# The low part of every fourth weight chunk made by an accumulating DMA instead of a VectorE subtraction

## The chip, the cores and the metric

The kernel runs on one core of a Trainium2 chip. The metric is the device time of one execution in microseconds (us). A core has a matrix engine (TensorE, PE in the profile; its weight loads are PEld), three engines for elementwise work (VectorE or DVE, ScalarE or ACT, GpSimd or POOL), and SyncE (SP), which here only issues DMAs. Every engine works through its own instruction stream in order. GpSimd and ScalarE can issue DMAs too. All DMAs of the core run on the same 16 DMA engines. TensorE writes into PSUM; everything else lives in SBUF, a memory of 128 partitions.

## The reference

One decoder layer on 256 rows of width 2048, in float32:

```
h = RMSNorm(x)
[cB|cC|cX|q|k|v|g_conv|g_attn] = h @ w_in                    # 2048 x 19456
A = (cB * causal_dwconv3(cC * cX)) @ w_conv_out              # 2048 x 2048
B = dilated_window_attention(rope(norm(q)), rope(norm(k)), v) @ w_attn_out   # 1024 x 2048
x = x + (sigmoid(g_conv) * A + sigmoid(g_attn) * B) @ w_merge_out            # 2048 x 2048
h = RMSNorm(x)
[g|u] = causal_dwconv3(h @ w_up)                             # 2048 x 11264
x = x + (silu(g) * u) @ w_down                               # 5632 x 2048
```

There are 24 heads of 128 in three groups of different dilation. The weights are 340 MB, all read once.

## The kernel before

**Two parts for each factor.** The products are made from float32r operands. Every weight and every activation is written as the sum of two float32r numbers, hi and lo, and each product takes three of the four combinations: hi by hi, hi by lo, lo by hi. For a weight chunk, hi is ScalarE's rounding of the raw float32 values to float32r (line 109), and lo is VectorE's difference raw minus hi (line 110).

**The weight stream.** All weights are one list of 656 chunks, numbered in the order in which TensorE uses them. A chunk is 512 KB, 4 KB in each partition (the first 16 are half of that). SyncE loads it into a buffer `raw` (line 99); there are 5 raw buffers. The split makes `whi` and `wlo`, with 4 buffers each (`SPLIT_BUFS`). While chunk i is at work, the program issues loads up to chunk i + 7 (`LOAD_AHEAD` of 8 counts the chunk itself) and splits up to chunk i + 2 (`SPLIT_AHEAD` of 3), but an instruction starts only when its buffer is free: hi of chunk i can be written when TensorE has read hi of chunk i - 4, and a raw buffer is loaded again when both split instructions of its chunk have read it.

**The products.** Chunks belong to blocks. A block of kind F has 256 weight columns and 4 chunks, and the weights stand in the array: per 128 rows and 128 columns one matmul with hi against both parts of the activations (line 185, 512 wide) and one with lo against their hi part (line 186, 256 wide). A block of kind T has 512 columns, 2 x 128 rows a chunk, and the weights stream past the activations in three matmuls (lines 189, 190 and 191; 190 uses lo). A block of kind T has 8 or 11 chunks; the attention-output blocks (F) have 2. Each block collects into one of two PSUM buffers and is then evacuated by ScalarE and VectorE (`fsum`, line 296 and 297), scaled, convolved, gated, and split for the next product.

**What sets the order.** The instruction order on each engine is put together by the framework's scheduler from the order in which the program issues work and its estimate of when inputs are ready. Work beside the stream (transposes, attention, convolution) is queued by `after(n, ...)` and issued n chunks later. In the up stage (blocks ug and uv, F) the convolution's two ScalarE instructions (line 311), the SiLU (line 614) and the split of the result (line 303) stand between the stream's instructions on ScalarE.

In the functions below `split_to` is the one that the change touches. `last["act"]` and `last["dve"]` hold the latest split instruction of each engine; `behind` uses them to issue side work after it.

Of the kernel before, what the change touches and what calls it, by code (L numbers as in the profile page):

```python
# [11 lines left out]
F32 = mybir.dt.float32  # L12
F32R = mybir.dt.float32r
I32 = mybir.dt.int32
AF = mybir.ActivationFunctionType
ALU = mybir.AluOpType
# [35 lines left out]
SPLIT_BUFS = 4  # L52
LOAD_AHEAD = 8
SPLIT_AHEAD = 3


def _round_bits(v, bits):
# [5 lines left out]
def hybrid_block(ctx: ExitStack, tc: tile.TileContext, x, positions, mix_norm, w_in, conv_mix_w,  # L63
                 w_conv_out, q_norm, k_norm, w_attn_out, w_merge_out, ffn_norm, w_up, ffn_conv_w,
                 w_down, out):
    nc = tc.nc
# [15 lines left out]
    def bank(name):  # L82
        return ps_one.tile([P, 512], F32, tag="one", name=name)

    # ---- the weight stream: chunks of rows by columns, 4 KiB a partition, loaded and split ahead.
    # A weight is the exact sum of two float32r parts, as the activations are.
    chunks, xt = [], []
    x_before = {min(2 * i, 13) for i in range(8)}
    raws, splits = {}, {}
# [2 lines left out]
    def load_to(n):  # L92
        while issued["load"] < min(n, len(chunks)):
            i = issued["load"]
            if i in x_before:
                xt.append(load_x(k2("x"), len(xt), FW))
            w, r0, kc, c0, cw = chunks[i]
            raws[i] = wpool.tile([P, kc, cw], F32, tag="raw", name="raw", bufs=RAW_BUFS)
            nc.sync.dma_start(raws[i], w[r0:r0 + kc * P, c0:c0 + cw].rearrange("(k p) n -> p k n", p=P))
            issued["load"] += 1  # L100

    def split_to(n):
        while issued["split"] < min(n, len(chunks)):
            i = issued["split"]
            load_to(i + 1)
            raw = raws.pop(i)
            hi = wpool.tile(list(raw.shape), F32R, tag="whi", name="whi", bufs=SPLIT_BUFS)
            lo = wpool.tile(list(raw.shape), F32R, tag="wlo", name="wlo", bufs=SPLIT_BUFS)
            last["act"] = nc.scalar.activation(hi, raw, AF.Copy)  # L109
            last["dve"] = nc.vector.tensor_tensor(lo, raw, hi.bitcast(F32), op=ALU.subtract)  # L110
            splits[i] = (hi, lo)
            issued["split"] += 1

    last = {}
# [28 lines left out]
    blocks, steps = [], []  # L143
# [10 lines left out]
    def interleave(n):  # L154
        half = n // 2
        for seq in (steps, chunks):
            head = seq[:n]
            seq[:n] = [head[i // 2 + (i % 2) * half] for i in range(n)]
            seq[n - 3], seq[n - 2] = seq[n - 2], seq[n - 3]

    def run_blocks():
        for i, (b, k, kc) in enumerate(steps):
# [8 lines left out]
            pump()  # L171
            load_to(i + LOAD_AHEAD)
            split_to(i + SPLIT_AHEAD)
            hi, lo = splits.pop(i)
            end = k + kc >= kts
# [16 lines left out]
            if end:  # L192
                b["evac"](ps)

    # ---- constants
    ident = cpool.tile([P, P], F32, name="ident")
    make_identity(nc, ident)
    ones = cpool.tile([P, P], F32, name="ones")
    nc.vector.memset(ones, 1.0)

    # the clock of TensorE rises while it works: it starts before the first data are there
    warm = ps_sc.tile([P, 4, S], F32, tag="sc", name="warm")
    for i in range(WARM):
        nc.tensor.matmul(warm[:, 0, :P], ones, ones, start=True, stop=True)
# [37 lines left out]
        nc.vector.tensor_copy(fconv.rearrange("p k c -> p (k c)"), tq[:, :264])  # L242
        nc.vector.tensor_copy(cols[:, 16:80], tq[:, 264:328])

    # ---- RMSNorm: rows' squares are summed here, 1/rms goes onto what the products give
    def row_squares(xs, ssq, c):
        junk = k2("junk")
        n = xs.shape[2]
        for t in range(NT):
            nc.scalar.activation(junk[:, :n], xs[:, t, :], AF.Square, accum_out=ssq[:, t, c:c + 1])  # L250
# [73 lines left out]
    X = [None] * 8  # L324
    x_src = src_of(X)

    # ---- branch A: the gated short convolution
    cy, m1 = [None] * 8, [None] * 8
    keep = {}

# [43 lines left out]
            nc.vector.tensor_tensor(m1[nb], m1[nb], gconv[nb], op=ALU.mult)  # L374
        return evac

    # ---- branch B: attention
    rot = {}

    def rope_tables():  # L380
# [190 lines left out]
                    n += 1 + t  # L571
        return evac

    # ---- merge, residual, feed-forward
    mg = [None] * 8

    def ev_attn_out(nb):
# [24 lines left out]
    act = {}  # L602
# [24 lines left out]
                nc.sync.dma_start(out_v[:, t, nb * CW:(nb + 1) * CW], x2[nb][:, t])  # L627
        return evac

    # ---- the order of the products  # L630
    W_in, W_co, W_ao, W_mo, W_up, W_dn = (w[0] for w in (w_in, w_conv_out, w_attn_out, w_merge_out, w_up, w_down))
    for nb in range(8):
        block(W_in, COL_CC + nb * FW, 0, KT, "F", x_src, ev_cc(nb), "cc", 4 if nb else 2)
# [32 lines left out]
        for nb in range(4):  # L666
            block(W_dn, nb * CW, b0 * FW, 2 * (b1 - b0), "T", a_src, ev_down(nb, b1 == NB), "dn")

    # ---- start: x comes in by columns between the weights of the first two blocks, whose steps
    # alternate, so that each piece of x serves both  # L670
    interleave(2 * KT // 2)
    ssq1 = cpool.tile([P, NT, 8], F32, name="ssq1")
    load_to(SPLIT_AHEAD)
    r1 = rb1 = None
# [5 lines left out]
    with tc.issue_after(first_gains().ins):  # L680
        split_to(1)
    h0, l0 = transposed(xt[0], 0, 0, X, "xT")
    with tc.issue_after(h0.ins), tc.issue_after(l0.ins):
        split_to(2)
# [33 lines left out]
```

## Time and profile before

| | |
|---|---|
| time, median of two runs | 1882.42 us (1882.35 to 1882.49) |
| span of the profiled execution, first to last instruction | 1874.8 us |
| mean granted TensorE clock in it | 0.998 |
| TensorE busy | 1864.8 us, 99% |
| TensorE weight loads busy (beside the matmuls) | 1595.4 us, 85% |
| VectorE busy | 1197.5 us, 64% |
| ScalarE busy | 936.8 us, 50% |
| GpSimd busy | 9.0 us |
| DMA: HBM read, share of the weight queue | 344.24 MB, 57.6% of 16 engines' time |

The profiled execution's own time is its span; what lies around the span is not recorded. A row of groups reads: line, engine, operation, output<-inputs, count | busy us, mean ns of one | idle us of the engine just before, and what ended it. A row of the timeline reads: start in us from the span's start, duration in us, engine, line, operation, and in brackets the idle time before it and what ended that. The matmuls are pipelined, so the distance from one start to the next is the better measure of one.

### The profile page before, as it was taken

The page shows a single profiled execution, that of the slowest core. Times are in us where ns is not written, and L with a number is a line of the kernel's source. Part 1 is how long each engine was busy: PE and PEld are TensorE (multiplying, and loading weights), DVE is VectorE, ACT ScalarE, POOL GpSimd, SP SyncE. Part 2 cuts the span into 40 slices and gives each one's busy share as a digit, 9 for nine tenths or more (in the row PEclk, how much of TensorE's full clock was granted, in tenths as well). Part 3 has the DMA queues.
Part 4 walks back from the last instruction along what each step waited for, and adds up shares of the span by engine and source line. Part 5 has one row for each costly group of instructions (what it writes and reads, how often), then busy time and mean ns, then how long its engine had stood idle before and what let it go on. Part 6 is the DMA issues. An engine that isn't in the chain of part 4 may idle for free.

```text
span 1874.8 us, 25347 instructions
## 1 busy us (share of the span) xinstructions
PE 1864.8 (99%) x9807; PEld 1595.4 (85%) x9807; DVE 1197.5 (64%) x1599; ACT 936.8 (50%) x1208; POOL 9.0 (0%) x24
## 2 busy tenths in 40 slices
PE   8999999999999999999999999999999999999998
PEld 7888888888888888888888888888888888888887
DVE  5776666555566575666476756777764467777643
ACT  6444444444555454555465545555553345555432
POOL 1000000000000000000000000000000000000000
PEclk9999999999999999999999999999999999999999
DMA  8555565656555644555545665655655565665563
GB/s 253 181 189 183 189 186 185 190 182 190 186 185 180 192 155 148 189 185 188 180 135 170 212 212 182 191 191 191 191 191 191 192 190 186 185 189 183 191 215 121
DMA packets 279480, 348.00 MB, mean 186 GB/s; under 512 B 10959, under 2 KB 209663, under 8 KB 279360
## 3 DMA queue, kind: packets, MB, share of 16 engines
q1 hardware_dynamic: 279104, 346.07, 57.6%
q8 instruction: 77, 1.26, 0.3%
q0 software_dynamic: 224, 0.30, 0.1%
q14 instruction: 43, 0.35, 0.1%
q10 hardware_dynamic: 32, 0.01, 0.0%
HBM read 344.24 MB, written 2.10 MB: 185 GB/s over the span
## 4 chain that ended last, share of the span: by engine, by line
PE 99%; DMA 0%; ACT 0%; SPq 0%; DVE 0%; DVEq 0%; issue 0%
PE ps_ug L185 9%; PE ps_uv L185 9%; PE ps_ug L186 4%; PE ps_uv L186 4%; PE ps_dn L190 4%; PE ps_dn L191 4%; PE ps_dn L189 4%; PE ps_cx L185 3%; PE ps_cc L185 3%; PE ps_co L185 3%; PE ps_gc L185 3%; PE ps_ga L185 3%; PE ps_cb L185 3%; PE ps_k L189 2%; PE ps_v L189 2%; PE ps_q L189 2%
## 5 line engine op out<-in xcount | busy, mean ns | idle before, releaser
L110 DVE TENSOR_TENSOR wlo<-raw,whi 128x1024 fp32r<-128x1024 f32 (+1 forms) x656 | 794.0, 1211 | 591.4 <-ACT whi L109 588.5
L109 ACT ACTIVATE whi<-raw 128x1024 fp32r<-128x1024 f32 (+1 forms) x656 | 688.0, 1049 | 840.0 <-PE ps_dn L191 134.3
L185 PE MATMUL ps_ug<-h,whi 128*128 128x512 f32 x704 | 247.5, 395 | 0.0
L185 PE MATMUL ps_uv<-h,whi 128*128 128x512 f32 x704 | 247.4, 395 | 0.0
L186 PE MATMUL ps_ug<-h,wlo 128*128 128x256 f32 x704 | 197.7, 281 | 0.0
L186 PE MATMUL ps_uv<-h,wlo 128*128 128x256 f32 x704 | 197.4, 280 | 0.0
L185 PEld LDWEIGHTS ps_uv<-h,whi 128*128 128x128 f32 x704 | 132.0, 187 | 30.9
L185 PEld LDWEIGHTS ps_ug<-h,whi 128*128 128x128 f32 x704 | 132.0, 187 | 30.9
L191 PE MATMUL ps_dn<-whi,act 128*128 128x512 f32 x352 | 137.0, 389 | 0.0
L189 PE MATMUL ps_dn<-whi,act 128*128 128x512 f32 x352 | 137.0, 389 | 0.0
L190 PE MATMUL ps_dn<-wlo,act 128*128 128x512 f32 x352 | 137.0, 389 | 0.0
L186 PEld LDWEIGHTS ps_ug<-h,wlo 128*128 128x128 f32 x704 | 133.0, 189 | 0.1
L186 PEld LDWEIGHTS ps_uv<-h,wlo 128*128 128x128 f32 x704 | 133.0, 189 | 0.0
L185 PE MATMUL ps_cc<-xT,whi 128*128 128x512 f32 x256 | 93.0, 405 | 0.1
L185 PE MATMUL ps_ga<-xT,whi 128*128 128x512 f32 x256 | 92.6, 402 | 0.0
L185 PE MATMUL ps_cx<-xT,whi 128*128 128x512 f32 x256 | 92.4, 403 | 0.2 <-ACT whi L109 0.2
L185 PE MATMUL ps_co<-conv,whi 128*128 128x512 f32 x256 | 90.8, 399 | 0.0
L185 PE MATMUL ps_gc<-xT,whi 128*128 128x512 f32 x256 | 90.8, 399 | 0.0
L185 PE MATMUL ps_cb<-xT,whi 128*128 128x512 f32 x224 | 79.5, 399 | 0.0
L189 PEld LDWEIGHTS ps_dn<-whi,act 128*128 128x128 f32 x352 | 66.1, 188 | 13.9
L190 PEld LDWEIGHTS ps_dn<-wlo,act 128*128 128x128 f32 x352 | 66.1, 188 | 13.7
L191 PEld LDWEIGHTS ps_dn<-whi,act 128*128 128x128 f32 x352 | 66.1, 188 | 13.6
(219 smaller groups left out, 3265.1 us busy)
## 6 DMA issues: line engine op xcount, KB each, us to landing
raw<-in_w_in SPq DMA_DIRECT2D x296, 512.0 KB, 3.5
raw<-in_w_up SPq DMA_DIRECT2D x176, 512.0 KB, 3.6
raw<-in_w_down SPq DMA_DIRECT2D x88, 512.0 KB, 4.0
raw<-in_w_conv_out SPq DMA_DIRECT2D x32, 512.0 KB, 3.5
raw<-in_w_merge_out SPq DMA_DIRECT2D x32, 512.0 KB, 3.5
raw<-in_w_attn_out SPq DMA_DIRECT2D x16, 512.0 KB, 3.5
raw<-in_w_in SPq DMA_DIRECT2D x16, 256.0 KB, 4.1
x<-in_x SPq DMA_DIRECT2D x8, 256.0 KB, 5.6
```

The source lines that it names most:

```text
L109: last["act"] = nc.scalar.activation(hi, raw, AF.Copy)
L110: last["dve"] = nc.vector.tensor_tensor(lo, raw, hi.bitcast(F32), op=ALU.subtract)
L185: nc.tensor.matmul(ps[:, m, :], hi[:, j, w_], xs, start=first, stop=False)
L186: nc.tensor.matmul(ps[:, m, :S], lo[:, j, w_], xs[:, :S], start=False, stop=last)
L189: nc.tensor.matmul(ps[:, m, :], sh, hi[:, j, :], start=first, stop=False)
L190: nc.tensor.matmul(ps[:, m, :], sh, lo[:, j, :], start=False, stop=False)
L191: nc.tensor.matmul(ps[:, m, :], sl, hi[:, j, :], start=False, stop=last)
```

## The change

From chunk 60 on, every chunk whose number is divisible by four gets its lo part in another way. ScalarE writes the negated rounding of raw into `wlo` (a second activation, with scale -1), and GpSimd issues a DMA from `raw` into `wlo` that adds to what is there: raw minus the rounding. VectorE's subtraction is left out for these chunks. Chunks 60, 64, ..., 652 are 149. In a block of kind F with four chunks it is always the first chunk of the block.

```
+DMA_FROM = 60
+DMA_EVERY = 4
...
             last["act"] = nc.scalar.activation(hi, raw, AF.Copy)
-            last["dve"] = nc.vector.tensor_tensor(lo, raw, hi.bitcast(F32), op=ALU.subtract)
+            if i >= DMA_FROM and i % DMA_EVERY == 0:
+                last["act"] = nc.scalar.activation(lo, raw, AF.Copy, scale=-1.0)
+                nc.gpsimd.dma_start(lo, raw, accum_op=ALU.add)
+            else:
+                last["dve"] = nc.vector.tensor_tensor(lo, raw, hi.bitcast(F32), op=ALU.subtract)
```

The rest of the diff takes out comments. The lines of the changed kernel are numbered 2 higher at the loads and the first split instruction (99 is 101, 109 is 111), the negated copy is 113, the DMA 114, the subtraction 116, and lines behind it are 6 higher (185 is 191, 311 is 317).

How the scheduler places the new instructions is shown at three places of the up stage. First ScalarE, from the evacuation of a ug block to that of the next uv block, before:

```order
L296 ACTIVATE upa<-ps_ug 128x512
L109 ACTIVATE whi<-raw 128x1024
L311 ACTIVATE upc<-up,fconv 128x256 x2
L109 ACTIVATE whi<-raw 128x1024
L614 ACTIVATE upc<-upc 128x512
L109 ACTIVATE whi<-raw 128x1024 x2
L296 ACTIVATE upa<-ps_uv 128x512
```

The same stretch of ScalarE in the changed kernel:

```order
L302 ACTIVATE upa<-ps_ug 128x512
L111 ACTIVATE whi<-raw 128x1024
L317 ACTIVATE upc<-up,fconv 128x256 x2
L113 ACTIVATE wlo<-raw 128x1024
L111 ACTIVATE whi<-raw 128x1024
L620 ACTIVATE upc<-upc 128x512
L111 ACTIVATE whi<-raw 128x1024 x2
L302 ACTIVATE upa<-ps_uv 128x512
```

The negated copy of the next block's first chunk does not follow its whi directly: the two convolution instructions stand between. Of the 149 copies 42 stand so, 90 follow their whi directly, and 17 have another instruction between, in ten of them the sigmoid of a gate (line 371).

Second TensorE, from the last matmul of a uv block into the next ug block, with what each instruction waits for (DVE: VectorE, Activation: ScalarE), before:

```order
L186 MATMUL ps_uv<-h_9757,wlo 128x256
L185 MATMUL ps_ug<-h_9228,whi 128x512 [waits DVE_49,Activation_49]
L186 MATMUL ps_ug<-h_9228,wlo 128x256 [waits DVE_49]
L185 MATMUL ps_ug<-h_9228,whi 128x512
L186 MATMUL ps_ug<-h_9228,wlo 128x256
```

And in the changed kernel, where DMASW stands for a DMA that GpSimd issued:

```order
L192 MATMUL ps_uv<-h_9841,wlo 128x256
L191 MATMUL ps_ug<-h_9306,whi 128x512 [waits DVE_49,Activation_49]
L192 MATMUL ps_ug<-h_9306,wlo 128x256 [waits DMASW3_49]
L191 MATMUL ps_ug<-h_9306,whi 128x512
L192 MATMUL ps_ug<-h_9306,wlo 128x256
```

TensorE's own order is the same; the second matmul of the block, the first with wlo, waits for the landing of the accumulation instead of VectorE.

Third SyncE, loads of w_up, before (DMAHW: the load that filled the buffer earlier):

```order
L99 DMA raw<-in_w_up 128x4x256 [waits DMAHW6_49,DVE_49]
L99 DMA raw<-in_w_up 128x4x256 [waits DMAHW7_49,DVE_49]
L99 DMA raw<-in_w_up 128x4x256 [waits DMAHW0_49,DVE_49]
L99 DMA raw<-in_w_up 128x4x256 [waits DMAHW1_49,DVE_49]
L99 DMA raw<-in_w_up 128x4x256 [waits DMAHW2_49,DVE_49]
```

And in the changed kernel:

```order
L101 DMA raw<-in_w_up 128x4x256 [waits DMAHW5_49,DMASW3_49]
L101 DMA raw<-in_w_up 128x4x256 [waits DMAHW7_49,DVE_49]
L101 DMA raw<-in_w_up 128x4x256 [waits DMAHW0_49,DVE_49]
L101 DMA raw<-in_w_up 128x4x256 [waits DMAHW2_49,DVE_49]
L101 DMA raw<-in_w_up 128x4x256 [waits DMAHW1_49,DMASW4_49]
```

Every fourth load now waits until an accumulation has landed, since that reads the raw buffer to its end, and the loads behind it on SyncE wait with it.

## The prediction

> **What bounds the kernel now.** First the page of the profile: busy time by engine, and the chain that ended last.
>
> ```profile
> span 1874.8 us, 25347 instructions
> PE 1864.8 (99%) x9807; PEld 1595.4 (85%) x9807; DVE 1197.5 (64%) x1599; ACT 936.8 (50%) x1208; POOL 9.0 (0%) x24
> PE 99%; DMA 0%; ACT 0%; SPq 0%; DVE 0%; DVEq 0%; issue 0%
> ```
>
> TensorE is busy for all but 10.0 us of the span and the chain is TensorE alone. Next, where those 10.0 us lie: stretches of the span, PE busy in the second column, DMA share next to last.
>
> ```profile
> 0.00:60.00 60.00, 54.80 (x299) 47.00 (x300) 38.85 (x65) 39.26 (x84) 6.29 (x19) 0.94 0.76 234
> 1116.00:1360.00 244.00, 244.00 (x1382) 213.91 (x1381) 177.78 (x234) 135.34 (x181) 0.00 (x0) 1.00 0.60 190
> 1730.00:1874.80 144.80, 139.98 (x643) 116.31 (x642) 74.58 (x78) 55.98 (x59) 0.00 (x0) 1.00 0.53 175
> ```
>
> 5.2 us stand at the start and 4.8 us at the end, so the stretch that the change touches has nothing to give back. VectorE and ScalarE are not the limit. The groups say how they stand idle:
>
> ```profile
> L110 DVE TENSOR_TENSOR wlo<-raw,whi 128x1024 fp32r<-128x1024 f32 (+1 forms) x656 | 794.0, 1211 | 591.4 <-ACT whi L109 588.5
> L109 ACT ACTIVATE whi<-raw 128x1024 fp32r<-128x1024 f32 (+1 forms) x656 | 688.0, 1049 | 840.0 <-PE ps_dn L191 134.3 <-PE ps_ug L185 94.0 <-PE ps_uv L185 86.1
> ```
>
> VectorE waits for ScalarE's whi; ScalarE waits for TensorE to finish with an older weight buffer. So the split runs a fixed distance ahead of TensorE. The timeline of an up block shows that distance.
>
> ```profile
> 1303.97 0.39 PE L185 MATMUL ps_uv<-h,whi 128*128 128x512 f32 x1
> ...
> 1306.83 1.06 ACT L109 ACTIVATE whi<-raw 128x1024 fp32r<-128x1024 f32 x1 [1.23 <-PE ps_uv L185]
> ...
> 1307.79 0.90 ACT L311 ACTIVATE upc<-up,fconv 128x256 f32<-128x256 f32 x2
> 1307.92 1.23 DVE L110 TENSOR_TENSOR wlo<-raw,whi 128x1024 fp32r<-128x1024 f32 x1 [0.22 <-ACT whi L109]
> ...
> 1309.65 1.06 ACT L109 ACTIVATE whi<-raw 128x1024 fp32r<-128x1024 f32 x1 [0.96 <-ACT upc L311]
> ...
> 1315.07 0.39 PE L185 MATMUL ps_ug<-h,whi 128*128 128x512 f32 x1
> 1315.07 0.19 PEld L186 LDWEIGHTS ps_ug<-h,wlo 128*128 128x128 f32 x1
> ```
>
> The uv block starts at 1303.97 and the next ug block at 1315.07: 11.10 us for four chunks, 2.78 us each. The whi that starts at 1306.83, when TensorE has left the first uv chunk, is for the first chunk of the ug block: with four buffers it refills the one just read. That is a chunk with a number divisible by 4, so it is one that the change touches. Its wlo is finished at 1309.15 and first loaded at 1315.07: **5.9 us of slack** behind VectorE. A block with less ScalarE work beside it:
>
> ```profile
> 403.95 1.06 ACT L109 ACTIVATE whi<-raw 128x1024 fp32r<-128x1024 f32 x1 [1.24 <-PE ps_gc L185]
> ...
> 412.35 0.40 PE L185 MATMUL ps_co<-conv,whi 128*128 128x512 f32 x1
> ```
>
> Here whi starts 8.40 us ahead of the use.
>
> **The change part by part.** Chunks 60, 64, ... 652 are 149 chunks. VectorE loses 149 x 1.211 = 180 us, ScalarE gains 149 x 1.06 = 158 us. Neither is on the chain, so both are worth nothing by themselves; ScalarE goes from 937 to 1095 us. What its extra instruction delays by 1.06 us is the next whi, which has 5.9 us of slack, and PSUM evacuations: there are two PSUM buffers, so a block's evacuation has until the next block ends, 11.1 us. Cost nothing.
>
> What can cost is the new chain for one chunk: whi, then the negated copy, then GpSimd's descriptors, then the transfer, and TensorE's first wlo load behind it. The window for the transfer, from issue to landing, is what the timeline leaves. In the plain case the copy starts 0.96 us after whi (as L311 does, 1306.83 to 1307.79) and ends 2.02 us after it: 8.40 - 2.02 - 0.03 (the wake-up from ScalarE's end at 1307.89 to VectorE's start at 1307.92) = **6.3 us**. In the order of the changed kernel 90 chunks are of this kind. In 42 chunks of the up stage the two L311 instructions stand between whi and the copy: they end at 1308.69, the copy starts 0.1 us before that and ends at 1309.65, window 1315.07 - 1309.65 - 0.03 = **5.4 us**. In 17 more something else stands there, mostly the gate's sigmoid:
>
> ```profile
> L365 ACT ACTIVATE gate<-gate 128x512 f32<-128x512 f32 x16 | 9.9, 621 | 0.4 <-DVE gate L364 0.4
> ```
>
> 6.3 less some 0.5 is **5.8 us** for them. TensorE stalls for what a transfer is longer than its window. It stalls anew at every touched chunk: the buffer that a touched chunk refills was the one of the touched chunk four earlier, so a stall gives no lead for the next.
>
> How long is the transfer? The trace of before has no accumulating DMA and none from SBUF to SBUF. Its nearest rows are DMA issues, with KB and us to landing, the queue's share, and GpSimd's own issue:
>
> ```profile
> q1 hardware_dynamic: 279104, 346.07, 57.6%
> raw<-in_w_up SPq DMA_DIRECT2D x176, 512.0 KB, 3.6
> gq<-in_q_norm POOLq DMA_DIRECT2D x1, 64.0 KB, 5.8
> prow<-in_ffn_norm POOLq DMA_DIRECT2D x1, 8.0 KB, 3.3
> pos<-in_positions POOLq DMA_DIRECT2D x1, 1.0 KB, 8.9
> 2.85 0.57 POOL L233 DMA_DIRECT2D gq<-in_q_norm  x1
> ```
>
> - Low end: a weight load of the same 512 KB, issued by SyncE, lands in **3.6 us**.
> - Fixed part for GpSimd: 8 KB land in 3.3 us, and those are hardly any data.
> - Data: 57.6% of 1874.8 us is 1080 us of all 16 engines for 346.07 MB, 3.12 us a MB, 1.64 us for 0.524 MB. An accumulation has two tensors to read, raw and the old wlo, for one written: I take two passes, 3.27 us.
> - High end: the slowest GpSimd row, **8.9 us**, which stood behind other issues in a stretch with more traffic (DMA share 0.76 against 0.60).
>
> I take 3.3 + 3.27 = **6.6 us**, near gq's 5.8 us, the row of 128 partitions issued by GpSimd. The stalls: 90 x 0.3 + 17 x 0.8 + 42 x 1.2 = 27 + 14 + 50 = **91 us**. At 3.6 us the sum is 0; at 8.9 us it is 90 x 2.6 + 17 x 3.1 + 42 x 3.5 = 234 + 53 + 147 = 434 us. Less than nothing is excluded: in that stretch TensorE has no idle time to lose.
>
> Two rules of the Trainium skill weigh on the data term; nothing here needs them. "DMA: Bandwidth & Descriptors", section "Anatomy of one DMA", fits a GpSimd copy as 2.0 us plus bytes over 436 GB/s, an estimate of 3.2 us for 512 KB: by it a single pass hides and the sum is 0. The 8 KB row, 3.3 us where it gives 2.0, stands against it. "Collectives: The Full Stack", Part 3, has an adding DMA read both operands on one ring at half the rate of a copy: by it the data term is two passes, as taken; no run here shows it.
>
> **What waits behind it.** On GpSimd only the next accumulation is queued, 11.1 us later. SyncE is another matter:
>
> ```profile
> SPq L99 <- DVE wlo L110: 1223.1, 539, 6.1
> ```
>
> It always stands waiting for a raw buffer. Now one load in four waits for the accumulation to land instead of VectorE, and the loads behind it in SyncE's queue with it. If the landing is at the start of the touched chunk, the freed buffer is needed, with five raw buffers, at the earliest by the whi that starts two chunks later, 5.6 us on; issue and landing take 3.6 us. That leaves 2 us, and a late whi has 5.9 us more. Cost nothing; it would cost if loads took over 9 us, and their slowest row below is just that, from the crowded start.
>
> ```profile
> DMA to landing us min/median/max: 2.8/3.5/9.4
> ```
>
> **The rivals.**
>
> *Hidden.* The transfer lands within its window: 6.2 us or less, where the sum is 90 x 0 + 17 x 0.4 + 42 x 0.8 = 40 us, about the 2% that a measurement of this kernel can tell from no change. For it: the 3.6 us of the weight load, with the same bytes. Against: gq's 5.8 us with an eighth of them. It gives 1882 us, up to 1922. Chance 0.33. The first rule above would bring it about.
>
> *Shared engines.* The transfer takes turns with the weight loads on the same 16 DMA engines, which are 60% taken. In 6 us there are two loads of 1.64 us: one in the way makes the transfer 8.2 us and the sum 90 x 1.9 + 17 x 2.4 + 42 x 2.8 = 330 us, two make it 9.9 us and 90 x 3.6 + 17 x 4.1 + 42 x 4.5 = 583 us. So 2212 to 2465 us. For it: gq's 5.8 us for 64 KB when the engines were crowded. Against: a stalled TensorE also takes its loads later, so they thin out. An addition that runs slower than a copy would look the same. Chance 0.27.
>
> *ScalarE in the way.* The copy starts late since ScalarE stands waiting for VectorE's input to L311. VectorE has 180 us less to do, so that input comes no later; the price is 42 x the delay, 42 us for 1 us. Chance 0.02, 1924 us.
>
> *Faster.* TensorE's 10.0 idle us lie at the start and the end, outside the touched chunks: 0.02 for what I do not see.
>
> That the change does nothing can be excluded: GpSimd's order has the 149 transfers.
>
> **How the numbers follow.** The span of 1874.8 us stands 7.6 us below the median of 1882.4; stalls add to both alike. Forecast, transfer between 6.2 and 7.9 us: 1882.4 + 91 = 1973 us, chance 0.36, its own range 1922 to 2167 (at 7.9 us 90 x 1.6 + 17 x 2.1 + 42 x 2.5 = 285 us). With 0.33 for hidden and half of "shared engines" the range reaches from 1880 to 2330 (the 8.9 us end: 1882 + 434 = 2316), leaving out some 0.17. Slower by over 2%: 0.36 + 0.27 + 0.02 = 0.65; within: 0.33; faster: 0.02.
>
> **What would show it.** The DMA issues of wlo with their time to landing, 6.6 us if I am right; idle time of TensorE before the first wlo matmul of a touched chunk, released by that DMA, 149 times with most in the up stage; PE busy unchanged near 1865 us; VectorE near 1017 us, ScalarE near 1095. Wrong if the landing is under 6 us, if TensorE waits for whi or raw instead, or if the waits do not repeat at every fourth chunk.

## The result and the profile after

The changed kernel takes 1901.78 us (1901.57 to 1902.00) against 1882.42 us (1882.35 to 1882.49): ratio 1.0103, 95% interval 1.0073 to 1.0132. It is slower by 19.4 us, clear of noise, but within 2%. By the spans of the two profiled executions the difference is 25.4 us (1900.2 against 1874.8). A timed execution takes 1.8 us more than its span (1902.0 against 1900.2), so the profiled one of before, with its span of 1874.8 us, was shorter than the two that were timed. In the sessions below the kernel before takes some 1878 us, and the ratios there are taken with that.

The page of the changed kernel, busy time and chain:

```profile
span 1900.2 us, 25631 instructions
PE 1870.3 (98%) x9807; PEld 1593.3 (84%) x9807; DVE 1027.3 (54%) x1450; ACT 1076.5 (57%) x1357; POOL 136.9 (7%) x173
PE 72%; DMA 10%; ACT 2%; issue 1%; DVE 0%; DVEq 0%
```

TensorE is busy as long as before (1870 against 1865 us), but idle for 30 us instead of 10, and the chain now runs through DMAs. The view of the waits says where TensorE stood:

```profile
PE ps_dn L196 <- DMA wlo<-raw: 8.6, 9, 1.9
PE ps_mo L196 <- DMA wlo<-raw: 6.8, 6, 2.2
...
PE ps_k L196 <- DMA wlo<-raw: 1.4, 2, 1.0
...
PE ps_v L196 <- DMA wlo<-raw: 0.7, 2, 0.4
PE ps_ug L192 <- DMA wlo<-raw: 0.4, 1, 0.4
PE ps_gc L192 <- DMA wlo<-raw: 0.3, 1, 0.3
```

It waits for the landing of the accumulation, as forecast, but 21 times and not 149 times, for 18.2 us in all. And it waits in the T blocks (ps_dn, ps_mo, ps_k, ps_v), hardly in the F blocks (ps_ug, ps_gc), where the forecast had the shortest windows. A wait costs some 0.3 us more than is listed: with the one of 1.03 us at 1822.63 us, TensorE took 12.20 us for four chunks instead of 10.88. So 21 waits are some 24 us (an estimate) of the 25.4 us between the spans. The DMA part of the page, queues (packets, MB, share of the 16 engines' time) and issues:

```profile
q1 hardware_dynamic: 279104, 346.07, 55.7%
q0 software_dynamic: 21680, 78.43, 21.7%
...
wlo<-raw POOLq DMA_DIRECT2D x149, 512.0 KB, 4.8
```

The median landing is 4.8 us, not 6.6. On the engines one accumulation is 0.217 x 1900.2 / 149 = 2.77 us, one load 0.557 x 1900.2 / 346.07 x 0.524 = 1.60 us. The accumulations issued in two stretches, 1136 to 1380 us (up, F) and 1760 to 1880 us (down, T):

```profile
DMA to landing us min/median/max: 4.7/4.7/7.2
...
DMA to landing us min/median/max: 4.4/7.3/9.1
```

So the same transfer lands 2.6 us later in T blocks. (A landing is counted from the issue. Below, the window is the time from the issue to the moment at which TensorE needs the wlo.) The timeline of one down-stage step shows what is around it (SPq with x4: four issues, and the time from the first to the last; only these rows are shown):

```profile
1810.44 2.41 SPq L101 DMA_DIRECT2D raw<-in_w_down  x4
...
1813.03 1.06 ACT L113 ACTIVATE wlo<-raw 128x1024 fp32r<-128x1024 f32 x1 [1.83 <-PE ps_dn L196]
1814.00 1.04 ACT L111 ACTIVATE whi<-raw 128x1024 fp32r<-128x1024 f32 x1
...
1814.38 0.86 POOL L114 DMA_DIRECT2D wlo<-raw  x1 [10.42 <-ACT wlo L113]
...
1822.63 0.50 PE L196 MATMUL ps_dn<-wlo,act 128*128 128x512 f32 x1 [1.03 <-DMA wlo<-raw]
1822.65 0.37 SPq L101 DMA_DIRECT2D raw<-in_w_down  x1
```

SyncE issues four loads in 2.4 us. The accumulation is issued 1.5 us behind the last of them, and is needed 1822.63 - 1.03 - 1814.38 = 7.2 us later; it lands after 8.2 us. Then the next loads leave, 12.2 us after the first of the last four. Here the copy (L113) stands ahead of its whi (L111). An up-stage step:

```profile
1343.31 0.86 POOL L114 DMA_DIRECT2D wlo<-raw  x1 [10.23 <-ACT wlo L113]
...
1345.37 5.87 SPq L101 DMA_DIRECT2D raw<-in_w_up  x4
```

Here the next load leaves 2.1 us behind the accumulation, the four are spread over 5.9 us, and the last load ahead of it left 3.5 us before, at 1339.78 us. And SyncE's waits of the whole run:

```profile
SPq L101 <- DVE wlo L116: 741.5, 284, 6.2
SPq L101 <- DMA wlo<-raw: 679.3, 148, 10.5
```

SyncE stands 679 us waiting for landings; before, it waited for VectorE nearly alone.

### The profile page after: what moved, and what is told of

The parts are those of the page before. It is cut to its first block, busy times and chain, and to the rows that moved or that the text cites. A ratio compares the mean times of both kernels' runs of the same rounds, so it can differ in the third digit from the quotient of the medians.

```text
span 1900.2 us, 25631 instructions
## 1 busy us (share of the span) xinstructions
PE 1870.3 (98%) x9807; PEld 1593.3 (84%) x9807; DVE 1027.3 (54%) x1450; ACT 1076.5 (57%) x1357; POOL 136.9 (7%) x173
## 3 DMA queue, kind: packets, MB, share of 16 engines
q1 hardware_dynamic: 279104, 346.07, 55.7%
## 4 chain that ended last, share of the span: by engine, by line
PE 72%; DMA 10%; ACT 2%; issue 1%; DVE 0%; DVEq 0%
DMA wlo<-raw 10%; PE ps_uv L191 9%; PE ps_ug L191 9%; PE ps_ug L192 4%; PE ps_uv L192 4%; PE ps_ga L191 3%; PE ps_dn L196 3%; PE ps_co L191 3%; PE ps_gc L191 3%; PE ps_dn L195 3%; PE ps_dn L197 3%; PE ps_q L195 2%; PE ps_q L196 2%; PE ps_q L197 2%; PE ps_v L196 2%; PE ps_v L195 2%
## 5 line engine op out<-in xcount | busy, mean ns | idle before, releaser
L111 ACT ACTIVATE whi<-raw 128x1024 fp32r<-128x1024 f32 (+1 forms) x656 | 687.6, 1048 | 655.8 <-PE ps_ug L191 89.2
L116 DVE TENSOR_TENSOR wlo<-raw,whi 128x1024 fp32r<-128x1024 f32 (+1 forms) x507 | 612.2, 1208 | 716.0 <-ACT whi L111 712.5
L114 POOL DMA_DIRECT2D wlo<-raw x149 | 127.8, 858 | 1611.7 <-ACT wlo L113 1503.2
L113 ACT ACTIVATE wlo<-raw 128x1024 fp32r<-128x1024 f32 x149 | 156.5, 1050 | 88.7 <-PE ps_dn L196 43.0
```

The source lines that it names most:

```text
L113: last["act"] = nc.scalar.activation(lo, raw, AF.Copy, scale=-1.0)
L114: nc.gpsimd.dma_start(lo, raw, accum_op=ALU.add)
```

## The experiments

Each ratio is against the kernel before in the same session. "Stalls" is the sum of TensorE's waits for an accumulation in the profiled execution, as read above (18.2 us in 21 for the changed kernel).

**Where it is.** f_only makes the change in F blocks alone, t_only in T blocks alone:

```
-            if i >= DMA_FROM and i % DMA_EVERY == 0:
+            if i >= DMA_FROM and i % DMA_EVERY == 0 and raw.shape[2] == FW:   # f_only; t_only: == CW
```

> The accumulation is kept only for chunks of blocks of kind F (1 KB rows in HBM); chunks of kind T are split by VectorE again. The traced stalls of the changed kernel (17 of its 18 us of TensorE waiting before a wlo matmul) lie in blocks of kind T or right behind them. Theory burst (a late accumulation holds SyncE's queue, four loads come out at once, and the next accumulation waits behind them in the DMA engines) and theory rows (loads in 2 KB rows take engine time from the accumulation) both expect 1882 to 1885 us. Theory ScalarE (the extra copy on ScalarE costs by itself everywhere) expects about 1893, about half of the loss, since half of the copies stay.

> The complement: the accumulation only for chunks of blocks of kind T. Burst and rows expect 1900 to 1902 us, the whole loss; ScalarE expects about 1892.

f_only: 1880.94 us, ratio 1.0011 (1.0000 to 1.0021), stalls 0.8 us. t_only: 1903.22 us, 1.0131 (1.0114 to 1.0148), stalls 18.8 us in 24. The whole loss is made in the T blocks. ScalarE's extra copies and VectorE's missing subtractions cost at most 0.2% in F blocks.

**Is it the waiting or the traffic?** In side_accum VectorE makes every lo as before, and GpSimd accumulates every fourth raw into a buffer that nobody reads (one work buffer fewer makes room for it):

```
+            last["dve"] = nc.vector.tensor_tensor(lo, raw, hi.bitcast(F32), op=ALU.subtract)
             if i >= DMA_FROM and i % DMA_EVERY == 0:
-                last["act"] = nc.scalar.activation(lo, raw, AF.Copy, scale=-1.0)
-                nc.gpsimd.dma_start(lo, raw, accum_op=ALU.add)
+                nc.gpsimd.dma_start(scr..., raw, accum_op=ALU.add)
```

> VectorE subtracts for every chunk as before; beside it GpSimd accumulates every fourth raw chunk from number 60 into a scratch tile of 4 KB that nobody reads (paid for by one work buffer). The traffic and the hold on the raw buffers stay, TensorE's wait for the landing is gone, and ScalarE's second instruction too. If the wait for the landing is the whole path of the loss, 1878 to 1884 us. If late loads cost by themselves, or the DMA traffic slows TensorE, over 1890 us.

One run: 1880.18 us, before 1878.19. The same 78 MB move beside the stream and TensorE does not slow down, so the traffic is not the price. SyncE's waiting is not tested by it: here the accumulation does not wait for ScalarE, and SyncE waits for landings for 55 us only.

**What the transfer costs.** side_mix puts four kinds in turn in that place: 512 KB added, 512 KB copied, 256 KB added, 256 KB copied.

```
+                if kind == 0: nc.gpsimd.dma_start(sv, raw, accum_op=ALU.add)
+                elif kind == 1: nc.gpsimd.dma_start(sv, raw)
+                elif kind == 2: nc.gpsimd.dma_start(sv[:, :h], raw[:, :h], accum_op=ALU.add)
+                else: nc.gpsimd.dma_start(sv[:, :h], raw[:, :h])
```

> As side_accum, but the transfers into the scratch tile go round in four kinds: 512 KB accumulated, 512 KB copied, 256 KB accumulated, 256 KB copied. Their times to landing price the transfer: my sum took 3.3 us fixed and 1.64 us for each of two passes over 512 KB. By it 6.6, 4.9, 4.9 and 4.1 us. If the accumulation is one pass at the price of a copy, the first equals the second, and the third the fourth.

One run, 1877.81 us. Issue and landing of the four lines, in the order above:

```profile
L119 POOL DMA_DIRECT2D scr<-raw x37: 858/864/917, 160.2 to 1813.3; - x37
...
DMA to landing us min/median/max: 4.8/6.0/7.1
...
L121 POOL DMA_DIRECT2D scr<-raw x37: 546/548/555, 171.9 to 1824.4; - x37
...
DMA to landing us min/median/max: 2.9/5.1/6.6
...
DMA to landing us min/median/max: 3.2/4.2/6.9
...
DMA to landing us min/median/max: 2.3/3.3/4.7
```

By the shortest landings 256 KB more cost 1.6 us when added and 0.6 us when copied, and GpSimd issues an addition in 0.86 us instead of 0.55. By the records of their packets 512 KB take 3.3 us of the engines when added and 1.6 us when copied, on average: two passes. In the changed kernel the shortest landing of the 149 is 4.4 us, of which 2.6 us lie between its first packet and its last; what is left, some 1.7 us, is the fixed part. The forecast's prices of 6.6, 4.9, 4.9 and 4.1 us are 1.7 to 2 us above the shortest landings. The medians are higher; here the transfers leave directly behind raw's loads.

**The first theory: a load held in SyncE's queue.** A load that waits for the landing holds those behind it, so that four leave together, ahead of the next accumulation. own_raws gives the touched chunks raw buffers of their own, two of the five:

```
+            own = i % DMA_EVERY == 0
-            raws[i] = wpool.tile(..., tag="raw", bufs=RAW_BUFS)
+            raws[i] = wpool.tile(..., tag="rawd" if own else "raw", bufs=2 if own else 3)
```

> All 149 accumulations stay. The five raw buffers are divided: two for chunks divisible by four, three for the others, so that the load which has to wait for a landing is the one eight chunks later, and no other load stands behind it in SyncE's queue. Burst expects the loads to come out one at a time, accumulations in the down stage to land in 4.5 to 5.5 us instead of 7 to 9, and 1882 to 1886 us. Rows expects landings of 7 us and more to stay in blocks of kind T and 1895 to 1902 us. ScalarE expects no change, 1902.

raw6_k4 has six raw buffers and one work buffer fewer:

```
-K4_BUFS = 24
+K4_BUFS = 23
-RAW_BUFS = 5
+RAW_BUFS = 6
```

> Six raw buffers instead of five, paid for by one of the 24 work buffers of 4 KB. Burst expects the load that waits for a landing to be one chunk later in its queue and so less pressing: stalls in the down stage mostly gone, 1883 to 1892 us. Rows expects 1895 to 1902 us, ScalarE 1902.

own_raws: 1903.39 us, 1.0128 (1.0113 to 1.0144), stalls 18.3 us. raw6_k4: 1906.08 us, 1.0158 (1.0129 to 1.0188), stalls 21.4 us. Both forecasts of the theory failed, and neither run refutes it: in own_raws the scheduler set the waiting load ahead of three loads that could have gone, and SyncE waits 671 us for landings as before. In raw6_k4 the load that waits is that of chunk k + 6 instead of k + 5 in the down stage (k is the accumulated chunk), but it is still the first of the loads that are held, and four leave together:

```profile
1817.47 1.90 SPq L101 DMA_DIRECT2D raw<-in_w_down  x4
```

The next accumulation, issued at 1821.45, lands after 8.1 us. The kernel own_raws_ord adds an order by chunks to own_raws:

```
+                with tc.issue_after(before.ins):
+                    last["load"] = nc.sync.dma_start(raws[i], ...)
```

> As own_raws (two raw buffers for chunks divisible by four, three for the others), and the loads are now held in the order of the chunks on SyncE. In own_raws the scheduler had put the load eight chunks on, which waits for the landing, ahead of three loads whose buffers were free, so the four still came out together. Burst expects the loads to come out one at a time now, landings in the down and merge stages of 4.5 to 6 us, no stall there, and 1877 to 1883 us beside a before of 1878. Rows (2 KB rows alone slow the accumulation) expects landings of 7 us and more and about 1900 us still.

1915.28 us, 1.0202 (1.0177 to 1.0227), stalls 25.5 us in 31. SyncE's waits and the landings there:

```profile
SPq L107 <- DVE wlo L122: 1369.3, 439, 9.9
...
wlo<-raw POOLq DMA_DIRECT2D x149, 512.0 KB, 5.5
```

No load waits for a landing any more, and the landings are longer. So a load held by a landing is not needed for the loss. In this form two loads leave close together right ahead of the accumulation: one that VectorE let go, and behind it the one into a buffer of its own, which had long been free.

**The second theory: the accumulation stands behind the loads that left before it.** The trace has for each accumulation the loads that were issued before it and had not landed. In the changed kernel, for the 12 accumulations between 800 and 942 us (11 of them in T blocks) there are 2.5 such loads on average, and the accumulation lands 2.50 us (median) behind the last of them; from 1136 to 1512 us the landing and that last load go together with a correlation of 0.96. The engines give it nothing before: of the one issued at 1803.10 the packets start at 1806.5, when the loads issued up to 1801.60 are nearly through; of the accumulation with the shortest landing they start 1.4 us after the issue. half_load takes bytes away from the loads (three T chunks of four bring their first half, and both halves are split from it, so the products are others):

```
+            if cw == CW and i >= DMA_FROM and i % DMA_EVERY:
+                nc.sync.dma_start(raws[i][:, 0], w[r0:r0 + P, c0:c0 + cw])
+                raws[i] = raws[i][:, :1].to_broadcast([P, kc, cw])
```

half_acc takes bytes away from the accumulation (VectorE subtracts the first half of a touched T chunk):

```
+                    last["act"] = nc.scalar.activation(lo[:, 1:], raw[:, 1:], AF.Copy, scale=-1.0)
+                    nc.gpsimd.dma_start(lo[:, 1:], raw[:, 1:], accum_op=ALU.add)
+                    last["dve"] = nc.vector.tensor_tensor(lo[:, :1], raw[:, :1], hi[:, :1].bitcast(F32), op=ALU.subtract)
```

rows1k makes each load of a T chunk in two loads of 256 columns:

```
+                for h in range(0, CW, FW):
+                    nc.sync.dma_start(raws[i][:, :, h:h + FW], w[...c0 + h:c0 + h + FW]...)
```

> In the T blocks three loads of four bring only the first half of their chunk, and both halves are split from it, so the products are others; the accumulated chunks are loaded whole. Theory 'queue' (the accumulation gets the DMA engines only when the loads issued ahead of it have landed, and lands about 2.5 us after the last of them): fewer bytes stand ahead, the landings in T blocks fall from the median of 6 to 8 us to 4.5 to 5.5 us, TensorE's stalls from 18 us to under 3 us, ratio to before 1.000 to 1.003. Rival 'held' (it is slow since SyncE waits for the landing, or the T blocks are late for a reason in their own order): the waits of SyncE are the same, so the stalls stay over 10 us, ratio over 1.006.

> In the T blocks only the second half of a touched chunk is accumulated (256 KB), VectorE subtracts the first half. Theory 'queue': the loads ahead are the same, the accumulation itself takes some 1.3 us less, so landings of 5 to 6.5 us in T blocks within a window of 7.2 us: stalls under 5 us, ratio 1.000 to 1.004. Rival 'held' or 'rows': the landing is set by the loads alone and hardly falls, stalls over 10 us, ratio over 1.006.

> Each load of a chunk of a T block is two loads of 256 columns, with rows of 1 KB as in the F blocks, the bytes the same. Theory 'rows' (loads with rows of 2 KB take more of the engines' turns than those of 1 KB): landings in T blocks fall to the 4.5 to 5 us of the F blocks, ratio under 1.004. Theory 'queue' (bytes ahead count, not their rows): landings and stalls as with the change, ratio 1.008 to 1.015.

half_load: 1884.56 us, 1.0032 (1.0020 to 1.0045), stalls 1.8 us; the landings of the two down stages have medians of 4.8 us. half_acc: 1880.61 us, 1.0013 (1.0003 to 1.0023), stalls 0.3 us. rows1k: 1941.53 us, 1.0342 (1.0316 to 1.0368), stalls 45.0 us in 41. Fewer bytes ahead of the accumulation take nine tenths of the stalls away with SyncE's waits for landings still there (585 us), so it is the bytes ahead that count; the ratio just misses the 1.003 expected (the last section has a reason for some tenths of a per cent). rows1k is far above what either theory expected and does not separate them: a step of the down stage now has eight issues, which take 5.8 us where four took 2.4, so the burst is longer. half_acc proves less than it looks: the second half is also needed later, so the window grew from 7.1 to 8.9 us as the landing fell.

wlo5 widens the window instead, with a fifth wlo buffer (and one work buffer fewer):

```
-SPLIT_AHEAD = 3
+SPLIT_AHEAD = 4
-            lo = wpool.tile(..., tag="wlo", name="wlo", bufs=SPLIT_BUFS)
+            lo = wpool.tile(..., tag="wlo", name="wlo", bufs=SPLIT_BUFS + 1)
```

> A fifth wlo buffer, with splits issued one chunk further ahead (and one work buffer fewer). The negated copy can start before TensorE has left the old lo part of the touched buffer, some 1.5 to 2.5 us earlier, so the window for the landing in T blocks grows from 7.2 to about 9 us. Theory 'queue' with the window as the price: landings stay at 5.5 to 8 us, stalls fall from 18 us to under 4 us, ratio 1.000 to 1.004. Rival: the loads move with it (the later loads wait for the same landing), the landing takes as much longer as it starts earlier, stalls over 10 us, ratio over 1.006.

1940.76 us, 1.0340 (1.0325 to 1.0355), stalls 42.4 us in 60, now in F blocks as well. The rival held: the window is some 9 us in most blocks, and so is the landing. In T blocks the median window grew from 7.1 to 9.0 us and the landing from 5.9 to 8.9, and the stalls stayed (18.5 us against 17.5). In F blocks (23.9 us against 0.7) the edit did two things, since the load that waits there came one place forward too, from chunk k + 6 to k + 5.

```profile
SPq L101 <- DMA wlo<-raw: 1244.8, 148, 10.6
...
wlo<-raw POOLq DMA_DIRECT2D x149, 512.0 KB, 9.2
```

An accumulation that is issued earlier is issued right behind the loads that the last landing let go, and lands behind them. This is a loop: a landing lets several loads go, four in the down stage above, the next accumulation stands behind them, and its landing lets the next four go. On the engines it holds 4 x 1.60 + 2.77 = 9.2 us of work, to which come issue and start of the first load; in the down stage above it took 12.2 us. TensorE takes 10.9 us for four T chunks. So where the loop is closed it, and not TensorE, sets the pace.

**What closes it.** copy_after_hi puts the negated copy always behind its whi:

```
+                with tc.issue_after(last["act"].ins):
                     last["act"] = nc.scalar.activation(lo, raw, AF.Copy, scale=-1.0)
```

> The negated copy always stands behind the whi of its chunk on ScalarE, also in the T blocks, where the change had it ahead; by that the accumulation is issued about 1 us later there, the window shrinks from 7.2 to 6.2 us, and one more load goes out ahead of the one that waits for the landing. Theory 'loop' (landing, then a burst of held loads, then the next accumulation behind that burst, longer than TensorE's four chunks; it closes since the accumulation is issued only 1.5 us behind a load): the accumulation now meets emptier engines and lands in 4.5 to 5.5 us in T blocks as in F blocks, stalls under 4 us, ratio 1.000 to 1.004. Rival 'window' (the landing of 6 to 8 us stays, only the window counts): the stalls grow by 1 us at each touched chunk of the T blocks, over 40 us, ratio over 1.018.

1887.63 us, 1.0043 (1.0031 to 1.0054), stalls 4.4 us in 4. The accumulation leaves 1.2 us later in T blocks (median window 5.8 us), and lands in time nearly always: the loop is open, and "window" fell. But this edit moved two things. In the changed kernel, in T blocks, the load that waits for the landing of chunk k is mostly that of chunk k + 5 (59 of 65); in F blocks, and here nearly everywhere, the pool of buffers gives chunk k + 5 the buffer of chunk k + 1, and it is the load of chunk k + 6 that waits. Two kernels complete the table: held_later hands out the buffers so, copies as in the changed kernel; copy_after_hi_first has the late copy, and chunk k + 5 waits everywhere.

```
+            at = free.pop(0)
+            free.append(at)
+            if i >= DMA_FROM and i % DMA_EVERY == 1:          # held_later alone
+                free[-2], free[-1] = free[-1], free[-2]
+            raws[i] = wpool.tile([P, kc, cw], F32, tag="raw%d" % at, name="raw", bufs=1)
+            with tc.issue_after(last["load"].ins) if i >= DMA_FROM else nullcontext():
                 last["load"] = nc.sync.dma_start(raws[i], ...)
```

> ScalarE's order as with the change (the negated copy ahead of whi in T blocks, accumulation issued early), but the raw buffers are handed out so that the load waiting for the landing stands one place later in SyncE's queue, behind a load that waits for VectorE only. If that place decides (the load in front of it leaves before the landing, so that three and not four loads are let go together): stalls under 5 us, ratio under 1.005. If the early issue decides (the accumulation is issued 1.5 us behind a load and queues behind it): stalls of 12 us or more, ratio over 1.007.

> The negated copy behind whi in all blocks, so the accumulation is issued about 1 us later in T blocks, but the load that waits for the landing stands first, as with the change, with four loads held behind it. If the place in SyncE's queue decides: four loads go out together at each landing, the loop closes, stalls of 12 us or more, and up to 40 us since the window is 1 us shorter, ratio over 1.007. If the issue time decides: landings of 4.5 to 5.5 us as in copy_after_hi, stalls under 6 us, ratio under 1.006.

held_later: 1885.58 us, 1.0038 (1.0025 to 1.0051), stalls 4.4 us in 5. copy_after_hi_first: 1911.20 us, 1.0186 (1.0159 to 1.0212), stalls 20.6 us in 27.

In the table, ratio and stalls, and behind them the stalls of the T blocks alone (in its F blocks the changed kernel has the load of chunk k + 6 waiting):

| | waiting load: chunk k + 5 | waiting load: chunk k + 6 |
|---|---|---|
| copy ahead of whi in T blocks | the change: 1.0103, 18.2 us, T 17.5 | held_later: 1.0038, 4.4 us, T 4.1 |
| copy behind whi | copy_after_hi_first: 1.0186, 20.6 us, T 10.2 | copy_after_hi: 1.0043, 4.4 us, T 4.1 |

The place of one load in SyncE's queue decides. The time of the copy matters in T blocks while that load stands first (17.5 against 10.2 us), and no longer when it stands second. The place counts by what stands in front of the waiting load, not by its number: in raw6_k4 the load of chunk k + 6 waits too, but in the step shown no load leaves between the accumulation and its landing, and four leave behind it. It also settles what rows1k left open: held_later keeps the rows of 2 KB and loses the stalls, and the F blocks of copy_after_hi_first have rows of 1 KB and gain some.

Here is held_later in the down stage:

```profile
1799.15 0.86 POOL L121 DMA_DIRECT2D wlo<-raw  x1 [10.02 <-ACT wlo L120]
...
1805.73 3.16 SPq L108 DMA_DIRECT2D raw<-in_w_down  x3
...
1808.68 1.06 ACT L120 ACTIVATE wlo<-raw 128x1024 fp32r<-128x1024 f32 x1 [1.43 <-PE ps_dn L203]
...
1810.03 0.86 POOL L121 DMA_DIRECT2D wlo<-raw  x1 [10.02 <-ACT wlo L120]
```

Three loads follow the landing, over 3.2 us, instead of four in 2.4; the fourth waits for VectorE alone and left at 1803.09, 3.9 us behind the accumulation before. The step is 1810.03 - 1799.15 = 10.88 us, TensorE's own. SyncE's waits for landings fall from 679 to 238 us:

```profile
SPq L108 <- DVE wlo L123: 1109.4, 359, 7.6
SPq L108 <- DMA wlo<-raw: 238.2, 142, 5.0
```

And with the waiting load first in F blocks too, the stalls come to F blocks, where the change had none (copy_after_hi_first):

```profile
PE ps_dn L202 <- DMA wlo<-raw: 7.3, 9, 1.9
PE ps_ug L198 <- DMA wlo<-raw: 5.1, 6, 1.2
PE ps_uv L198 <- DMA wlo<-raw: 4.0, 5, 1.6
```

So the first theory was right for the changed kernel, and too narrow as a rule: what counts is how many loads have left and not landed when the accumulation is issued. In F blocks there are 1.2 of them on average in the changed kernel and 2.0 in copy_after_hi_first; in T blocks 2.6 in the changed kernel, 2.2 in held_later and 1.4 in copy_after_hi. A held queue is one way to get many, own_raws_ord shows another.

## Why the prediction was right and wrong

- **What bounds the kernel, and what was costed at nothing on the engines: right.** TensorE's wait for the landing is nearly the whole cost. VectorE lost 170 us (180 forecast) and ScalarE gained 140 (158), both for next to nothing (f_only in F blocks; held_later, with all 149 copies, is at 1.0038).
- **The transfer, 6.6 us: mis-sized.** Its median landing is 4.8 us, at its shortest 4.4, so the prediction is wrong by its own first sign (a landing under 6 us). The data term was near (3.27 forecast, 2.77 measured, 3.3 in side_mix); the fixed part of 3.3 us, read from GpSimd's 8 KB row, was twice too large (1.7). That this row comes from the crowded start of the kernel is the likely reason; it was not tested. The page "DMA: Bandwidth & Descriptors" of the Trainium skill (section "Anatomy of one DMA"), set aside for that row, fits 3.2 us for a GpSimd copy of 512 KB; the shortest copy in side_mix took 2.9. The page "Collectives: The Full Stack" of the Trainium skill, Part 3, has an adding DMA at two passes: side_mix agrees, with 3.3 us on the engines against 1.6 for a copy of the same bytes.
- **The windows: right in F blocks, wrong in T blocks.** In the up stages the trace has medians of 5.4 and 5.5 us (5.4 forecast), in the F blocks up to 460 us 6.1 (6.3). But "90 copies follow their whi directly" was a wrong count of the order, in the section on the change and in the sum: 37 do; 59 have one to three other instructions between, and 53, nearly all in T blocks, stand ahead of their whi. There the window is 7.1 to 7.2 us, not 6.3. The median landing is 4.7 us in F blocks and 5.9 in T blocks, both inside these windows, so by the prediction's own rule all three terms (27 + 14 + 50) come to zero.
- **SyncE, "Cost nothing": this step failed, and the loss is here.** It asked only whether a late load makes whi late, and found 2 + 5.9 us of slack; no whi was late. That four held loads leave together and stand ahead of the next accumulation, whose landing then holds the next four, was not seen. The runs put 17.5 us of the 18.2 us of stalls into T blocks, where this happens, and 4.1 us when the waiting load stands one place later (held_later). The rival "shared engines" had the mechanism (one load in the way is 1.6 us more) but gave it to every touched chunk, since it did not ask when the loads leave.
- **"It stalls anew at every touched chunk": wrong.** 21 stalls in 149. A chunk in an F block hardly ever stands behind a burst (2 of the 21 stalls), and a T block needs some steps until the landings have grown past the window.
- **The outcome** lies in the case called hidden (1882 to 1922 us), with a mechanism of the case called shared engines. The forecast of 1973 us was 71 us too high. That the range and the direction held is luck: the sum that gave the direction comes to zero, and the loss comes from a step that was priced at nothing. "Slower by over 2%", which had 0.65, did not come.

## What to carry to other kernels

Here the DMA that TensorE waits for landed as late as the loads issued in the microseconds before it let it. So cost such a DMA with those loads in front, and ask what its landing lets go: if that stands ahead of the next such DMA, there is a loop with a period of its own, to be set against the step of the engine. Which buffer the next load takes, and so which load in an in-order queue waits first, can decide whether the loop closes. A wider window need not help: in the T blocks of wlo5 the landing grew with it. And take the fixed cost of a DMA from a stretch with the traffic of the place in question, not from the start of the program.

## What the hardware showed that was not expected

TensorE runs the same F block in one of two steady steps. The prediction's rows of before have up blocks at 1303.97 and 1315.07 us, 11.10 us apart, at a granted clock of 1.00; held_later, with no wait between them:

```profile
1303.48 0.40 PE L198 MATMUL ps_ug<-h,whi 128*128 128x512 f32 x1
...
1314.79 0.40 PE L198 MATMUL ps_uv<-h,whi 128*128 128x512 f32 x1
```

That is 11.31 us, with the clock at 1.00 too. A stage mostly keeps the step it begins with, for 20 blocks and more; the T blocks of the down stages have one step only, 10.88 us. In the changed kernel the step changed at the first stall, at 312 us, from 11.3 to 11.1; in f_only the same stall left it at 11.3, and a later one, at 1329 us, changed it from 11.1 to 11.3. For the 21 blocks of the first up stage the two steps differ by 21 x 0.21 = 4.4 us; before and the changed kernel have the short one there, f_only for the first 15 blocks or so, held_later, copy_after_hi, half_acc and half_load the long one. So two or three tenths of a per cent in the ratios above can be this, and not the edit: held_later's 7.4 us can be 4.4 us of stalls and the rest of the long step. What sets the step was not tried.

Behind a long stall TensorE's clock can be lower for a while. Behind the longest wait of ps_dn, 1.9 us up to 1871.96 us, the granted clock (PEclk, third from the end) is 0.50 for 3.4 us:

```profile
1872.50:1875.90 3.40, 3.40 (x9) 2.64 (x8) 0.00 (x0) 0.00 (x0) 0.00 (x0) 0.50 0.74 222
```

Matmuls start 427 ns apart there instead of 227, which makes this wait some 1.6 us dearer (an estimate from the two spacings). The length of the wait alone does not decide it: behind the wait of 2.2 us in ps_mo the clock stayed at 1.00.
